# A 32 KB tile of normed activations moved from behind the weight buffers to the other end of SBUF

## The chip, the core and the metric

The kernel runs on one core of a Trainium2 chip, as one launch. The metric is the device time of that launch in microseconds. Three runs of the kernel before the change took 1527.56, 1529.47 and 1529.0 us; their median is 1529.0 us.

## What is computed

One decoder layer over 256 tokens of width 2048, in float32, cut to what matters here:

```
h    = RMSNorm(x)
proj = h @ w_in          # GDN q|k|v, beta, decay, out-gate z; attention q|k|v; gates A, B
y_a  = gated_deltanet(...) @ w_branch_a
y_b  = block attention(...) @ w_branch_b
x    = x + (sigmoid(gate_a) * y_a + sigmoid(gate_b) * y_b) @ w_out
h    = RMSNorm(x)
u    = causal_dwconv(h @ w_up)          # 2 x 5632 channels
x    = x + (silu(u_gate) * u_val) @ w_down
out  = RMSNorm(x)
```

Nearly all the arithmetic lies in the products with the weights: `w_in`, `w_branch_a`, `w_branch_b`, `w_out`, `w_up`, `w_down`.

## The kernel before

Activations stand transposed: channels on the 128 partitions, the 256 tokens along the free axis. Every float32 operand is split into a high and a low part in the type fp32r, and a product is the sum of high x high, high x low and low x high.

Weights come in blocks of 128 x 2048 numbers (1 MB). `fetch` (L120) lets SP issue the DMA into one of four `wraw` buffers; `load_w` (L125) lets ACT write the high part into one of two `wh` buffers (`split`, L118) and DVE the low part into one of two `wl` buffers (L115). These eight buffers of 8 KB in each partition are the pool `wpool`.

`block` (L168) multiplies a block of weights with an activation tile of the form [128, 16, 2, 256] (k-step, high or low, token). All its matmuls are issued at L108, in two forms:

- **Wide** (the gates from the fifth chunk on, the branches, the output projection, the up projection): for each k-step one matmul with `wh` as the stationary operand and the 512 columns high|low of the activations as the moving one, then one with `wl` and the 256 high columns. These two are called a pair below.
- **Narrow** (GDN, z, the attention's q and k, the first four gate chunks): three matmuls of 256 columns for each k-step.

Two products go the other way round, with the weights as the moving operand, 512 columns a time: the attention's v (`ps_v`, stationary `hc`) and the down projection (`pd`, L96, stationary `ah` and `al`, 128 columns a time).

The stages follow each other in this order: GDN, z and attention products with the delta rule and the attention running between them (`tick`, L103); gates (`ps_gate`); branches (`ps_br`, moving operands `yca` and `ycb`); output projection (`ps_wo`, moving operand `mc`); up projection (`ps_up`, moving operand `h2`); down projection (`pd`). The instructions are put in order by a scheduler when the program is built.

The tile in question is `hc` of the pool `hp` (L219, L220): 16 k-steps x 2 x 256 numbers, 32,768 bytes in each partition. It holds the normed input from the start until the gates are done. Under the same tag, and so at the same address, it is then `h2`, the normed input of the up projection, and at the very end `tail`, which holds the last two weight blocks of the down projection. The trace calls it `hc`, `h` and `tail`.

Pools stand as two stacks in SBUF. Without an argument a pool is put on the left stack, which grows upwards from low addresses: `keep`, `wpool`, `hp`, then `fk`, `m`, later `mp` (which holds `mc`), `b`, `b2` (which holds `ah`, `al` and the small tiles of the up projection). With `side="right"` it is put on the right stack, which grows downwards from the top: `n1`, `g`, `gp`, `yp` (`yca`, `ycb`), `bkeep`, `ak`.

## Time and profile before

| what | value |
|---|---|
| median of three runs | 1529.0 us (1527.56 to 1529.47) |
| span of the profiled execution | 1528.1 us |
| TensorE matmul (PE) busy | 1504.4 us, 98% |
| VectorE (DVE), ScalarE (ACT), GpSimd (POOL) busy | 67%, 49%, 12% |
| mean granted TensorE clock over the span | 0.997 |
| chain that ended last | PE 93%, of it `ps_up` 33%, `pd` 16%, `ps_gate` 11% |

The profile gives one execution, by its span from the first to the last instruction; that span is 0.9 us under the median of the three runs. Ends of matmuls are modelled in it and overlap the next one, so how fast matmuls follow each other is read from their starts, or from a long stretch and the number of matmuls in it. "PEld" is the load of a stationary operand.

### The profile page before, as it was taken

The numbers are of one execution on the slowest core, as the hardware profiler recorded it, in microseconds if no ns is written. First come the engines' busy times: TensorE is split into PE (matmuls) and PEld (weight loads), VectorE is DVE, ScalarE is ACT, GpSimd is POOL, SyncE is SP. The second block draws the span as 40 slices with busy tenths as digits, with TensorE's granted clock in tenths as the row PEclk, the third lists the DMA queues.
The fourth block names the chain that finished last, engine by engine and source line by source line (L and its number), as shares of the span: only waits on it lengthen the run. The fifth ranks groups of instructions, "written<-read, shape, count | busy, mean of one in ns | idle before, by whom it ended". The sixth has DMA issues, their size and how long they took to land.

```text
span 1528.1 us, 22511 instructions
## 1 busy us (share of the span) xinstructions
PE 1504.4 (98%) x9179; PEld 1343.1 (88%) x9179; DVE 1028.1 (67%) x1453; ACT 754.5 (49%) x1026; POOL 184.3 (12%) x137
## 2 busy tenths in 40 slices
PE   7999999999999999999999999999999999999997
PEld 6999999998998888888888888888888888888886
DVE  7887786886765555777766666766666676555554
ACT  5565463434474444445455545555455455444444
POOL 3001111041121000110101111111111111000000
PEclk9999999999999999999999999999999999999999
DMA  8454444444336553568545555555455554555552
GB/s 306 151 185 164 174 146 148 173 146 166 139 112 217 179 183 124 177 217 308 193 168 191 193 183 183 185 193 189 173 189 193 187 182 175 193 196 194 194 194 84
DMA packets 45639, 276.94 MB, mean 181 GB/s; under 512 B 5504, under 2 KB 6992, under 8 KB 15456
## 3 DMA queue, kind: packets, MB, share of 16 engines
q1 hardware_dynamic: 43712, 270.98, 49.8%
q0 software_dynamic: 960, 2.36, 0.6%
q10 hardware_dynamic: 864, 2.16, 0.4%
q8 instruction: 72, 1.18, 0.3%
q14 instruction: 31, 0.25, 0.0%
HBM read 271.68 MB, written 3.80 MB: 180 GB/s over the span
## 4 chain that ended last, share of the span: by engine, by line
PE 93%; DVE 4%; ACT 1%; issue 1%; DMA 0%; SPq 0%; DVEq 0%; ACTq 0%
PE ps_up L108 33%; PE pd L96 16%; PE ps_gate L108 11%; PE ps_gdn L108 9%; PE ps_wo L108 6%; PE ps_br L108 5%; PE ps_moba L108 4%; PE ps_z L108 3%; PE ps_v L108 3%; DVE wl L115 2%; ACT wh L118 1%; PE g L96 1%; PE py L545 1%; PE pu L551 1%; DVE tm L515 0%
## 5 line engine op out<-in xcount | busy, mean ns | idle before, releaser
L115 DVE TENSOR_TENSOR wl<-wraw,wh 128x1024 fp32r<-128x1024 f32 (+1 forms) x508 | 612.5, 1239 | 265.8 <-ACT wh L118 264.4
L118 ACT CAST wh<-wraw 128x1024 fp32r<-128x1024 f32 (+1 forms) x508 | 501.9, 1032 | 394.1 <-PE ps_up L108 126.8
L108 PE MATMUL ps_up<-h,wh 128*128 128x512 f32 x1408 | 497.9, 399 | 0.0
L108 PE MATMUL ps_up<-h,wl 128*128 128x256 f32 x1408 | 395.4, 281 | 0.0
L108 PEld LDWEIGHTS ps_up<-h,wh 128*128 128x128 f32 x1408 | 264.6, 188 | 66.1
L108 PEld LDWEIGHTS ps_up<-h,wl 128*128 128x128 f32 x1408 | 266.0, 189 | 0.1
L108 PE MATMUL ps_gate<-hc,wh 128*128 128x512 f32 (+1 forms) x640 | 183.1, 353 | 0.0
L108 PE MATMUL ps_gdn<-hc,wh 128*128 128x256 f32 x768 | 146.3, 291 | 7.5 <-ACT wh L118 5.8
L108 PE MATMUL ps_gate<-hc,wl 128*128 128x256 f32 x512 | 144.6, 282 | 0.6 <-DVE wl L115 0.6
L778 POOL TENSOR_TENSOR acts<-sg,cvf 128x256 f32<-128x256 f32 x44 | 80.8, 1837 | 432.6 <-ACT sg L777 432.6
L108 PEld LDWEIGHTS ps_gdn<-hc,wh 128*128 128x128 f32 x768 | 124.2, 198 | 8.5 <-ACT wh L118 5.8
L96 PE MATMUL pd<-wl,ah 128*128 128x512 f32 x336 | 130.8, 389 | 0.0
L96 PE MATMUL pd<-wh,al 128*128 128x512 f32 x336 | 130.8, 389 | 0.0
L108 PEld LDWEIGHTS ps_gate<-hc,wh 128*128 128x128 f32 x640 | 112.2, 189 | 18.0
L108 PE MATMUL ps_gdn<-hc,wl 128*128 128x256 f32 x384 | 111.7, 291 | 3.7 <-DVE wl L115 3.7
L772 ACT ACTIVATE cvf<-unf,ffv 128x256 f32<-128x256 f32 x88 | 48.2, 595 | 104.6 <-DVE unf L199 104.6
L774 DVE SCALAR_TENSOR_TENSOR cvf<-unf,ffv,cvf 128x254 f32<-128x254 f32 (+1 forms) x176 | 77.2, 480 | 32.2 <-ACT cvf L772 31.7
L108 PEld LDWEIGHTS ps_gate<-hc,wl 128*128 128x128 f32 x512 | 97.0, 189 | 0.8 <-DVE wl L115 0.8
L108 PE MATMUL ps_moba<-hc,wh 128*128 128x256 f32 x512 | 95.1, 285 | 0.0
L96 PE MATMUL pd<-wh,ah 128*128 128x512 f32 x336 | 92.8, 391 | 0.0
L108 PE MATMUL ps_wo<-mc,wh 128*128 128x512 f32 x256 | 88.8, 391 | 0.0
L108 PEld LDWEIGHTS ps_moba<-hc,wh 128*128 128x128 f32 x512 | 80.1, 191 | 0.2
(426 smaller groups left out, 2004.9 us busy)
## 6 DMA issues: line engine op xcount, KB each, us to landing
wraw<-in_w_up SPq DMA_DIRECT2D x88, 1024.0 KB, 4.8
wraw<-in_w_dn SPq DMA_DIRECT2D x44, 1024.0 KB, 4.8
wraw<-in_w_gate SPq DMA_DIRECT2D x32, 1024.0 KB, 4.8
wraw<-in_w_gdn SPq DMA_DIRECT2D x30, 1024.0 KB, 4.9
wraw<-in_w_moba SPq DMA_DIRECT2D x16, 1024.0 KB, 4.8
wraw<-in_w_o SPq DMA_DIRECT2D x16, 1024.0 KB, 4.8
wraw<-in_w_mv SPq DMA_DIRECT2D x8, 1024.0 KB, 4.8
wraw<-in_w_ba SPq DMA_DIRECT2D x16, 512.0 KB, 3.4
```

The costliest lines, as they stand in the source:

```text
L96: pe.matmul(ps, a, b, start=(start and i == 0), stop=(stop and i == n - 1), **kw)
L108: pe.matmul(ps, a, b, start=start, stop=stop, skip_group_check=True)
L115: (eng or dve).tensor_tensor(lo, src, hi.bitcast(F32), op=ALU.subtract)
L118: act.copy(hi, src)
L545: pe.matmul(py[:, p], ats[p], Tm[:, p], start=True, stop=True)
L551: pe.matmul(pu[:, p], Y[:, p, :], odd(U)[:, p], start=True, stop=True)
L772: act.activation(t[:, j, :], un[:, j, :], AF.Identity, scale=w[:, 2:3], bias=w[:, 3:4])
L774: dve.scalar_tensor_tensor(t[:, j, d:], un[:, j, :T - d], w[:, 2 - d:3 - d], t[:, j, d:], op0=ALU.mult, op1=ALU.add)
L778: pool.tensor_tensor(acts[:, c, :], sg, t[:, 1, :], op=ALU.mult)
```

## The change

The pool `hp` is put on the right stack, as the first pool there.

```diff
     hst = ExitStack()
-    hp = hst.enter_context(tc.tile_pool(name="hp", bufs=1))
+    hp = hst.enter_context(tc.tile_pool(name="hp", bufs=1, side="right"))
     hc = hp.tile([P, KD, 2, T], F32R, name="hc", tag="hc")
     hh, hl = hc[:, :, 0, :], hc[:, :, 1, :]
```

The other lines of the diff are comments that become empty lines; line numbers stay.

Both programs hold the same instructions in the same order on each engine, with the same waits. What differs are addresses. The pools that stood above `hp` on the left move down by its 32,768 bytes, and so do all pools of the right stack, which now begin below it. In bytes from the start of a partition:

| pool | tiles that matter here | before | after |
|---|---|---|---|
| `wpool` | `wraw` x4, `wh` x2, `wl` x2 | 18,624 to 84,160 | the same |
| `hp` | `hc`, `h2`, `tail` | 84,160 to 116,928 | 196,576 to 229,344 |
| `mp` | `mc` | 116,928 to 149,696 | 84,160 to 116,928 |
| `yp` | `yca`, `ycb` | 157,664 to 190,432 | 124,896 to 157,664 |
| `b2` | `ah`, `al` | 127,168 to 138,432 | 94,400 to 105,664 |
| `gp` | `gts` | 196,576 to 229,344 | 163,808 to 196,576 |

`wh` and `wl` lie at 51,392 to 84,160 in both programs. Every distance between two tiles stays what it was, except those to `hp` and, for tiles above it, those to `keep` and `wpool`.

## Rows read from the trace of the kernel before

**Rows 1.** Section 1 of the profile page: span, and busy time of each engine.

```profile
span 1528.1 us, 22511 instructions
PE 1504.4 (98%) x9179; PEld 1343.1 (88%) x9179; DVE 1028.1 (67%) x1453; ACT 754.5 (49%) x1026; POOL 184.3 (12%) x137
```

**Rows 2.** The chain of work that ended last, in order of time: start us, length us, engine, output tile, line, number of instructions.

```profile
347.73 10.00 PE ps_v L108 x44
...
455.13 141.46 PE ps_gate L108 x814
...
689.52 88.75 PE ps_wo L108 x512
779.14 4.86 PE ps_up L108 x28
784.86 492.54 PE ps_up L108 x2788
1285.77 234.67 PE pd L96 x1035
```

**Rows 3.** Busy time of each engine in 400 us of the up projection: stretch, its length, then PE, PEld, DVE, ACT and POOL, each with busy us and number of instructions, granted TensorE clock, DMA share, GB/s.

```profile
800.00:1200.00 400.00, 400.00 (x2266) 346.75 (x2265) 270.98 (x354) 205.64 (x286) 66.87 (x36) 1.00 0.52 187
```

**Rows 4.** The same view of 70 us of the output projection.

```profile
700.00:770.00 70.00, 70.00 (x405) 61.75 (x404) 49.89 (x54) 35.01 (x47) 7.47 (x5) 1.00 0.62 229
```

**Rows 5.** Groups of matmuls by shape: line, engine, output<-inputs, stationary, moving, count | busy us, mean ns of one (its end modelled) | idle us before them.

```profile
L108 PE MATMUL ps_up<-h,wh 128*128 128x512 f32 x1408 | 497.9, 399 | 0.0
...
L108 PE MATMUL ps_gate<-hc,wh 128*128 128x512 f32 x384 | 135.7, 399 | 0.0
...
L108 PE MATMUL ps_wo<-mc,wh 128*128 128x512 f32 x256 | 88.8, 391 | 0.0
...
L108 PE MATMUL ps_br<-yca,wh 128*128 128x512 f32 x128 | 44.7, 390 | 0.0
```

**Rows 6.** Timeline of PE in the up projection, the wide matmuls of four consecutive pairs and, three pairs on, one more: start us, modelled length us.

```profile
849.71 0.40 PE L108 MATMUL ps_up<-h,wh 128*128 128x512 f32 x1
...
850.05 0.40 PE L108 MATMUL ps_up<-h,wh 128*128 128x512 f32 x1
...
850.40 0.40 PE L108 MATMUL ps_up<-h,wh 128*128 128x512 f32 x1
...
850.77 0.40 PE L108 MATMUL ps_up<-h,wh 128*128 128x512 f32 x1
...
851.83 0.40 PE L108 MATMUL ps_up<-h,wh 128*128 128x512 f32 x1
```

**Rows 7.** The same for the output projection, four consecutive pairs.

```profile
739.63 0.39 PE L108 MATMUL ps_wo<-mc,wh 128*128 128x512 f32 x1
...
739.98 0.39 PE L108 MATMUL ps_wo<-mc,wh 128*128 128x512 f32 x1
...
740.33 0.39 PE L108 MATMUL ps_wo<-mc,wh 128*128 128x512 f32 x1
...
740.67 0.39 PE L108 MATMUL ps_wo<-mc,wh 128*128 128x512 f32 x1
```

**Rows 8.** Timeline of PE where the gates end and the branches begin.

```profile
595.02 0.40 PE L108 MATMUL ps_gate<-hc,wh 128*128 128x512 f32 x1
...
596.08 0.40 PE L108 MATMUL ps_gate<-hc,wh 128*128 128x512 f32 x1
...
596.43 0.40 PE L108 MATMUL ps_br<-yca,wh 128*128 128x512 f32 x1
...
596.78 0.39 PE L108 MATMUL ps_br<-yca,wh 128*128 128x512 f32 x1
...
597.82 0.39 PE L108 MATMUL ps_br<-yca,wh 128*128 128x512 f32 x1
```

**Rows 9.** Timeline of PE in a narrow stage, the attention's q and k: the last matmul of three consecutive k-steps (each has three matmuls of 256 columns).

```profile
260.12 0.28 PE L108 MATMUL ps_moba<-hc,wl 128*128 128x256 f32 x1
...
260.48 0.28 PE L108 MATMUL ps_moba<-hc,wl 128*128 128x256 f32 x1
...
260.84 0.28 PE L108 MATMUL ps_moba<-hc,wl 128*128 128x256 f32 x1
```

**Rows 10.** Timeline of PE in the product v where it is slowest: every third matmul.

```profile
278.24 0.39 PE L108 MATMUL ps_v<-wl,hc 128*128 128x512 f32 x1
...
278.94 0.39 PE L108 MATMUL ps_v<-wl,hc 128*128 128x512 f32 x1
...
279.63 0.39 PE L108 MATMUL ps_v<-wl,hc 128*128 128x512 f32 x1
...
280.32 0.39 PE L108 MATMUL ps_v<-wl,hc 128*128 128x512 f32 x1
```

**Rows 11.** One line of ACT, the copy of a 128x512 result out of PSUM into tiles of three pools: count, least/median/greatest ns, first and last start.

```profile
L196 ACT COPY unf<-ps_up x44: 571/577/580, 793.0 to 1279.2; 128x512 f32<-128x512 f32 x44
L196 ACT COPY bt<-ps_br x15: 573/580/582, 603.1 to 684.3; 128x512 f32<-128x512 f32 x15
L196 ACT COPY gts<-ps_gate x12: 573/579/581, 474.0 to 597.5; 128x512 f32<-128x512 f32 x12
```

## The prediction

> **What bounds the kernel now.** I read the busy times first: the matmul engine is busy 1504.4 of 1528.1 us, the next engine, DVE, 1028.1 [rows 1]. Then the chain that ended last: gates, output projection, up projection and down projection stand on it as long unbroken pieces of matmuls [rows 2]. [...] So the weights arrive in time there, and what counts is how fast one matmul follows the last. The change adds, removes and reorders no instruction; only if an address sets that pace can it move the time.

> So I compared the pace of stages that issue the same pair of matmuls, 512 columns with `wh`, then 256 columns with `wl`. From the chain [rows 2]: the up projection runs 2788 matmuls, 1394 pairs, in 492.54 us, **353.3 ns a pair**; the output projection 512 matmuls, 256 pairs, in 88.75 us, **346.7 ns a pair**. The groups by shape show the same seam: the 512-column matmul lasts 399 ns by the profile where the moving operand is `hc` or `h`, and 390 or 391 where it is `mc` or `yca` [rows 5]. The starts show how it comes about. In the up projection pairs follow each other after 0.34, 0.35 and 0.37 us, 1.06 us for three, and again 1.06 for the next three [rows 6]; in the output projection after 0.35, 0.35 and 0.34 us, 1.04 us for three [rows 7]. The seam lies at the tile, not at a pause: the last three gate pairs take 1.06 us (595.02 to 596.08), then the moving operand changes from `hc` to `yca` with PE running on, and three pairs from 596.78 to 597.82 take 1.04 us [rows 8].

> What is different between those stages? The weight buffers are the same, the shapes are the same, and the output projection has the other engines and the DMA about as busy (DVE 49.9 of 70 us, DMA share 0.62 against 0.52) [rows 3, 4]. What is left is the moving operand's place: `hc` and `h2` at 84,160, right behind `wpool`; `mc`, `yca` and `ycb` at 116,928 and above. The trace shows no cause beyond that, and one row speaks against it: the first 28 matmuls of the up projection, 14 pairs with `h2` at the same address, took 4.86 us, 347.1 ns a pair, up to 784.0 us, where a norm's matmuls step in and the slower pace begins [rows 2]. The place may only make the slow pace possible, and the way a stage is entered then decide.

> **The change part by part.** The profiled execution is the base: its span of 1528.1 us.

> *`hc` and `h2` at 196,576.* In the wide stages they are the moving operand of 1394 pairs of the up projection and of 384 pairs of the gates (x384 in [rows 5]). The least each can cost is the pace of `mc`, 346.7 ns; no row shows a faster pair, and the down projection's 512-column matmul (234.67 us for 1035, 226.7 ns [rows 2]) with the narrow stages' 256-column one (0.36 us for three, 120 ns [rows 9]) also add up to 346.7. The most is every pair as slow as the slowest of the three, 0.36 to 0.37 us by starts given to 0.01 us [rows 6]; at 0.36 that is 6.7 ns more than now, +11.9 us on 1778 pairs. I take the pace of `mc` and `yca`, because they are two tiles at two other places and both have it, and `ycb`, up to 190,432, is the nearest to the new place. That gives 1394 x 6.65 ns = 9.3 us and 384 x 6.65 ns = 2.5 us, together **-11.8 us**, all on the chain.

> *`mc` at 84,160, where `hc` was.* I charge it what `hc` pays there: 256 pairs x 6.65 ns = **+1.7 us**; ends 0 and, at 0.36 us a pair, +3.4.

> *`ah` and `al` at 94,400.* They are the stationary operand of the down projection's 1056 matmuls, with the weights moving, and now lie where `hc` lay. The nearest row is v, with `hc` stationary and the weights moving. At its slowest it took 2.08 us for nine matmuls, 231.1 ns [rows 10]; in a longer piece 10.00 us for 44, 227.3 ns [rows 2], which is the down projection's pace of today but for rounding. I take **0**; the bad end is 1056 x 4.4 ns = +4.7 us.

> *v and the narrow stages.* v has 192 matmuls with `hc`; between its two paces lie 192 x 4.4 ns = 0.8 us either way. The narrow stages already run at 120 ns, the floor worked out above, so I take **0** for them.

> *Everything else that moves.* ACT, DVE, POOL and DMA work with tiles 32,768 bytes lower. ACT's copy takes a median of 577, 580 and 579 ns into `unf` (left stack), `bt` and `gts` (right stack) [rows 11]: the place does not show. This work also lies beside PE. If PE gains 1.9% in the up projection, DVE's 271 us fall on 392 us instead of 400, and the output projection shows that weights can come faster (229 against 187 GB/s [rows 3, 4]), so the gain is not turned into a wait: **0**.

> Sum: -11.8 + 1.7 = -10.1 us, a span of 1518.0 us. The median of the runs is 0.9 us above the span of the profiled execution, so I predict **1519 us**. With the ends of `mc` and v in its favour it would be 1516.5; with the down projection's bad end 1523.7.

> [...]

> **The rivals.**

> *The place has no say.* The two paces would then be two ways in which the same stream of matmuls can run, chosen by how a stage begins. For it: the 347.1 ns at the start of the up projection, from the same address. Against it: the pace changes at `hc` to `yca` without a pause [rows 8], and the 1394 pairs after that start keep one pace for 492 us. Since the program's instructions and their order stay, each stage keeps its pace: 1529. [...]

> *The place allows it, the entry decides.* Then gates and up projection can part company at the new address. If only the up projection gets the fast pace, 1529 - 9.3 + 1.7 = 1521.4; if only the gates do, 1529 - 2.5 + 1.7 = 1528.2.

> *Slower: what moves in behind the weights pays, and `hc` is not relieved.* If the top of SBUF suits `hc` no better than its old place, nothing is gained, but `mc` pays 1.7 us and `ah` and `al` up to 4.7: 1529 + 6.4 = 1535.4. It decides once the down projection loses over 1.4 us (1.3 ns a matmul), since 1.7 + 1.4 is 0.2% of the time. Against it stand `yca` and `mc`, both fast at higher addresses, and v's return to 227 ns. If `hc` were to run worse there, up to 11.9 us would come on top.

> **How the numbers follow.** About 0.2%, 3 us, is what a measurement of this kernel can tell from no change. The forecast gets 0.58, the place without a say 0.24, the mixed case 0.08, half of it faster and half the same, the slower case 0.10. That makes faster 0.62, same 0.28, slower 0.10. The forecast's own range is 1516.5 to 1523.7. It holds too little alone; up to 1530, just above the slowest of the three runs, it takes in the cases of no change and the mixed ones, and leaves out the slower case: **1516.5 to 1530**.

> **What would show it.** Right: `ps_up` and `ps_gate` at 346.7 ns a pair, their 512-column matmul at 390 or 391 ns instead of 399, the piece of 2788 matmuls on the chain at about 483.3 us instead of 492.5; `ps_wo` up at 353 ns, 90.4 us for its 512; `pd` still at 226.7 ns. Wrong: `ps_up` still at 353.3 ns and 399 ns; or PE gaining there and idle before `ps_up` on `wl` by DVE, which would make DVE the bound I ruled out; or `pd` at 228 ns and more. Were `ps_up` relieved and `ps_wo` unchanged, the old place would not have been the cause, or not alone.

## The result: 1512 us, 1.1% faster than before

The changed kernel took 1512.2 us (median; 1511.06 to 1512.97), the kernel before 1529.1 us on the same chip; the ratio is 0.9894 (95% interval 0.9879 to 0.9908). The prediction was 1519 us with a range of 1516.5 to 1530: right in the sign and in the size of its largest term, but the gain that it gave is 7 us too small. Two executions in the whole record, 3829 us of the kernel before and 3008 us of e6_left128, were disturbed and stand in no ratio.

The profiled execution after the change has a span of 1510.8 us, 17.3 less than before. This is its page, as [rows 1]:

```profile
span 1510.8 us, 22511 instructions
PE 1487.7 (98%) x9179; PEld 1337.7 (89%) x9179; DVE 1027.2 (68%) x1453; ACT 754.6 (50%) x1026; POOL 184.9 (12%) x137
```

All of it is PE's: its busy time falls by 16.7 us, DVE's by 0.9. The chain after the change, beside [rows 2] (start us, length us, number of instructions):

```profile
105.33 11.20 PE ps_z L108 x96
...
342.42 10.25 PE ps_v L108 x44
...
449.36 138.81 PE ps_gate L108 x814
...
681.18 88.75 PE ps_wo L108 x512
770.80 4.86 PE ps_up L108 x28
776.52 483.26 PE ps_up L108 x2788
1268.14 235.03 PE pd L96 x1035
```

Read the starts against [rows 2]. The wide gates' piece starts 5.8 us earlier (455.13 to 449.36), the output projection 8.3 us earlier (689.52 to 681.18), the long piece of the up projection still 8.3 (784.86 to 776.52), the down projection 17.6 (1285.77 to 1268.14). So 5.8 us come from the stages before the wide gates, 2.6 from the wide gates and the branches, 0 from the output projection, 9.3 from the up projection, and the end gives 0.3 back. The 2788 matmuls of the up projection take 483.26 us, 346.7 ns a pair; the 96 of z take 11.20 us, 116.7 ns each. In the chain before, the same 96 took 120.0 ns each:

```profile
107.70 11.52 PE ps_z L108 x96
```

The groups by shape, as [rows 5], agree:

```profile
L108 PE MATMUL ps_up<-h,wh 128*128 128x512 f32 x1408 | 488.6, 390 | 0.0
...
L108 PE MATMUL ps_gate<-hc,wh 128*128 128x512 f32 x384 | 133.2, 390 | 0.0
```

And the narrow stage of [rows 9] on the timeline (start us, length us, engine, line), three k-steps of three matmuls each:

```profile
254.89 0.28 PE L108 MATMUL ps_moba<-hc,wl 128*128 128x256 f32 x1
...
255.24 0.28 PE L108 MATMUL ps_moba<-hc,wl 128*128 128x256 f32 x1
...
255.59 0.28 PE L108 MATMUL ps_moba<-hc,wl 128*128 128x256 f32 x1
...
255.94 0.27 PE L108 MATMUL ps_moba<-hc,wl 128*128 128x256 f32 x1
```

Here 0.35 us pass from k-step to k-step where 0.36 passed before.

### The profile page after: what moved, and what is told of

It is laid out like the page before. It is cut to its first block, busy times and chain, and to the rows that moved or that the text cites. A ratio compares the mean times of both kernels' runs of the same rounds, so it can differ in the third digit from the quotient of the medians.

```text
span 1510.8 us, 22511 instructions
## 1 busy us (share of the span) xinstructions
PE 1487.7 (98%) x9179; PEld 1337.7 (89%) x9179; DVE 1027.2 (68%) x1453; ACT 754.6 (50%) x1026; POOL 184.9 (12%) x137
## 4 chain that ended last, share of the span: by engine, by line
PE 93%; DVE 4%; ACT 1%; issue 1%; DMA 0%; POOL 0%; SPq 0%; DVEq 0%; ACTq 0%
PE ps_up L108 32%; PE pd L96 16%; PE ps_gate L108 11%; PE ps_gdn L108 9%; PE ps_wo L108 6%; PE ps_br L108 5%; PE ps_moba L108 4%; PE ps_z L108 3%; PE ps_v L108 3%; DVE wl L115 2%; ACT wh L118 1%; PE g L96 1%; PE py L545 1%; PE pu L551 1%; DMA wraw<-in_w_gdn 0%
## 5 line engine op out<-in xcount | busy, mean ns | idle before, releaser
L108 PE MATMUL ps_up<-h,wh 128*128 128x512 f32 x1408 | 488.6, 390 | 0.0
L108 PE MATMUL ps_gate<-hc,wh 128*128 128x512 f32 (+1 forms) x640 | 179.6, 347 | 0.0
L118 ACT CAST ah<-acts 128x256 fp32r<-128x256 f32 x44 | 17.9, 407 | 125.8 <-PE pd L96 116.1
```

The lines of the kernel that those rows point to most:

```text
L108: pe.matmul(ps, a, b, start=start, stop=stop, skip_group_check=True)
L118: act.copy(hi, src)
```

## The experiments

All kernels but one are the layer with unused bytes put ahead of or behind a tile; instructions and their order on each engine are the same in all of these. `pad(stack, name, bytes)` allocates a pool that nobody uses. The theory I held after seeing the result is A: not the place of `hc` counts but its start modulo a small number of bytes, relative to the weights. Before, `hc` and the weights start at the same value modulo 64 (and 256); after, `hc` starts 32 past them. P is the prediction's theory, that the place right behind the weights is to blame.

### e1_left32, hc stays behind the weights, 32 bytes on

```diff
-    hst = ExitStack()
-    hp = hst.enter_context(tc.tile_pool(name="hp", bufs=1))
+    hst = ExitStack(); pad(hst, "pa", 32)
+    hp = hst.enter_context(tc.tile_pool(name="hp", bufs=1)); pad(hst, "pb", 32)
```

> The kernel before, with 32 unused bytes ahead of hc and 32 behind it: hc stays on the left stack right behind the weight buffers, but starts at 84,192, which is 32 modulo 64, as the changed kernel's 196,576 is (before: 84,160, 0 modulo 64). All other tiles keep their start modulo 64; instructions and order stay. Theory A (the start modulo 64 decides): as the changed kernel, 1512 us, up projection 346.7 ns a pair, narrow matmuls 117 ns, v 233 ns. Theory P (the place behind the weights decides): as before, 1529 us, 353.3 ns, 120 ns, v 227 ns. Theory D (the distance from hc to the weight buffers, before a multiple of 8,192, decides): 1512 us as well, so e3 has to part it from A.

Measured: 1519.7 us, ratio 0.994 (0.9925 to 0.9955). Its chain (columns as above, and so in the chains below):

```profile
104.24 11.20 PE ps_z L108 x96
...
679.95 90.42 PE ps_wo L108 x512
...
776.96 483.25 PE ps_up L108 x2788
1268.61 241.38 PE pd L96 x1035
```

z and the up projection run as in the changed kernel, with `hc` still right behind the weights: P falls. But the time is not 1512 us, since two other stages lost: `ps_wo` 1.7 us, `pd` 6.3 (233.2 ns a matmul instead of 227.1). The two pads had moved `mc`, `ah` and `al` by 64 bytes, which I had taken for harmless. So 64 bytes count too, for other tiles as well.

### e2_right0, hc at the far end, 0 modulo 64

```diff
+    hst = ExitStack(); pad(hst, "pa", 32, side="right")
+    hp = hst.enter_context(tc.tile_pool(name="hp", bufs=1, side="right")); pad(hst, "pb", 32, side="right")
```

> The changed kernel, with 32 unused bytes ahead of hc and 32 behind it on the right stack: hc stays at the far end but starts at 196,544, 0 modulo 64. All other tiles keep their start modulo 64. Theory A: as the kernel before, 1529 us, 353.3 ns a pair in gates and up projection, narrow 120 ns, v 227 ns. Theory P: as the changed kernel, 1512 us. Theory D: 1512 us, since 196,544 is not a multiple of 8,192 away from the weights.

Measured: 1530.9 us, ratio 1.001 (0.9987 to 1.0033); three of its ten executions took 1521.4 to 1524.1 us, and the profile shows none of these. Its chain:

```profile
106.72 11.52 PE ps_z L108 x96
...
612.67 8.40 PE ps_br L108 x46
...
624.41 8.26 PE ps_br L108 x46
...
688.83 90.45 PE ps_wo L108 x512
780.14 4.86 PE ps_up L108 x28
785.87 492.54 PE ps_up L108 x2788
```

At the far end, but with the old start modulo 64, the old pace is back: 492.54 us, to the last digit that of [rows 2], and z at 120.0 ns. A holds, P is wrong on this side too. One row is new: `mc` lies at 84,160 here as it does in the changed kernel, with the same weights, and takes 90.45 us instead of 88.75. So the same two addresses give both paces.

### e3_left64, hc behind the weights, 64 bytes on

```diff
+    hst = ExitStack(); pad(hst, "pa", 64)
     hp = hst.enter_context(tc.tile_pool(name="hp", bufs=1))
```

> The kernel before, with 64 unused bytes ahead of hc: 84,224, still 0 modulo 64 and behind the weights, but no longer a multiple of 8,192 away from them. Theory A: 1529 us, 353.3 ns and 120 ns. Theory P: 1529 us. Theory D: 1512 us, 346.7 ns and 117 ns.

Measured: 1532.2 us, ratio 1.0032 (1.0017 to 1.0047). None of the three theories had it: z takes 11.31 us for 96 matmuls, 117.8 ns; the gates run at 348.9 ns a pair, the up projection at 353.3, and `pd`, whose `ah` and `al` moved by 64 as well, loses 6.3 us against the changed kernel. The chain:

```profile
105.96 11.31 PE ps_z L108 x96
...
451.14 139.66 PE ps_gate L108 x814
...
780.83 492.55 PE ps_up L108 x2788
1281.77 241.36 PE pd L96 x1035
```

Modulo 64 is therefore too short a rule; theory D (a multiple of 8,192) is out.

### e4_w32, the weights moved by 32 bytes

```diff
+    wst = ExitStack(); pad(wst, "pa", 32)
+    wpool = wst.enter_context(tc.tile_pool(name="wpool", bufs=2)); pad(wst, "pb", 32)
```

> The kernel before, with 32 unused bytes ahead of the weight buffers and 32 behind them: weights start at 32 modulo 64, hc at 84,224 (0 modulo 64). Theory A in its relative form (moving and stationary tile must start 32 apart modulo 64): gates and up projection 346.7 ns, narrow 117 ns, a gain of about 18 us there; the branches (yca and ycb at 32, as the weights now) may go from 346.7 to 353.3 ns, +1.7 us; v and the down projection, weights moving at 32 and stationary at 0, from 227 to 233 ns, +1.2 and +6.7 us; about 1520 us in all. Theory A in its absolute form (the moving tile's own start decides): hc as before, 353.3 and 120 ns; the weights as moving operand are now at 32, so v and the down projection may change in either direction; 1522 to 1536 us. Theories P and D: 1529 us and, by D, 1512 us.

Measured: 1519.3 us, ratio 0.9938 (0.9923 to 0.9953), as A's relative form had it. `hc`, at the same 84,224 as in e3_left64, is fast in the wide stages once the weights start 32 bytes before it modulo 256 (up projection 483.26 us against 492.55), so the distance between the two operands counts, not either start. `pd` loses 6.2 us (241.25 us). The narrow stages did not quite follow: these 96 matmuls of z take 11.31 us, 117.8 ns each, as in e3_left64, where 117 was expected.

```profile
104.93 11.31 PE ps_z L108 x96
```

The branches, whose operands are now 0 apart modulo 256, show in the chain how one distance had two paces:

```profile
587.64 13.77 PE ps_br L108 x79
604.80 8.40 PE ps_br L108 x46
616.54 8.41 PE ps_br L108 x46
628.34 8.27 PE ps_br L108 x46
640.07 8.27 PE ps_br L108 x46
```

Between these pieces PE waits a moment for `wl`, 0.29 us ahead of the one at 604.80. After one wait the same 46 matmuls take 8.40 us, after another 8.27, and no piece of 46 in this chain has a length between. The 0.13 us are 5.7 ns for each of the 23 pairs, most of the 6.6 between 353.3 and 346.7 ns. So my estimate, from these lengths, is that here the pace was chosen when the stream started again and kept nearly to the next stop. In [rows 8] it changes with the operands, 1.06 us for three pairs before and 1.04 after.

### b1_offsets, TensorE alone

```diff
+    rev(ws[0], 3)
+    for w in ws:
+        wide(w, 6)
+        narrow(w, 4)
+        rev(w, 6)
+    for w in ws:
+        narrow(w, 2)
+        wide(w, 6)
```

> Not the layer: TensorE alone, which runs the layer kernel's three kinds of product on 15 pairs of weight tiles that differ only in where they start, 0 to 224 bytes past a multiple of 256, while the activation tile stays at 128 past one. Output is a placeholder. For each pair: 48 wide pairs (512 and 256 columns, activations moving), 96 narrow matmuls (256 columns), 48 with the weights moving (512 columns); then in a second pass 48 narrow and 48 wide pairs again, so that wide is entered from another state. Theory A in its relative form (the distance from the stationary to the moving tile modulo 128 decides; runs of the layer so far: 0, 32 and 64): weights at 0 and at 128 give the same, wide 346.7 or 353.3 ns depending on how it is entered, narrow 120, weights moving 227; weights at 96 (activations 32 ahead) wide 346.7, narrow 117; weights at 64 wide 349 to 353, narrow 118, weights moving 233; distances under 32 bytes are open. If the distance modulo 256 counts, weights at 0 and 128 differ. Theory P (the place in SBUF decides): no pattern in the offset, a trend with the address, since the tiles lie one after the other from 49 KB to 180 KB.

Of the new kernel only the order of its products is shown. `ws` holds the 15 pairs of weight tiles; `wide`, `narrow` and `rev` issue the three forms, the last with the weights moving. The kernel leaves out all else of the layer, and its output means nothing. It ran once.

Worked out from the starts of the matmuls in the last two thirds of each group, to about 0.2 ns; d is the activations' start less the weights', modulo 256:

| d | wide pair, ns: pass 1, 2 | narrow, ns: pass 1, 2 | weights moving, ns |
|---|---|---|---|
| 0 | 353.6, 346.7 | 120.0, 120.0 | 226.7 |
| 16 | 346.7, 346.7 | 117.4, 119.9 | 236.8 |
| 32 | 346.7, 346.7 | 116.7, 116.7 | 233.3 |
| 48 | 350.0, 350.0 | 116.7, 116.7 | 230.0 |
| 64 | 353.4, 348.8 | 117.8, 117.8 | 233.4 |
| 80 | 349.2, 349.1 | 118.1, 118.1 | 231.2 |
| 96 | 350.0, 350.0 | 120.1, 119.9 | 234.3 |
| 104 | 350.1, 349.9 | 116.7, 117.9 | 233.4 |
| 112 | 349.2, 349.3 | 120.0, 120.0 | 233.3 |
| 120 | 348.9, 349.0 | 118.1, 118.0 | 233.3 |
| 124 | 353.4, 353.4 | 120.1, 118.7 | 236.0 |
| 128 | 351.2, 351.2 | 118.6, 119.9 | 232.2 |
| 160 | 346.6, 346.6 | 117.3, 118.7 | 233.3 |
| 192 | 353.4, 353.3 | 117.8, 113.4 | 233.4 |
| 224 | 353.6, 353.6 | 118.4, 118.4 | 233.3 |

The 5784 matmuls of the run stand on its chain as one unbroken piece of 935.33 us, and most paces of the layer are there at their distance: 0 (before), 32 (after), 64 (e3_left64, with both of its paces), 224 (the pieces of 8.40 us in the branches of e2_right0, whose pairs of 346 and 361 ns have a mean of 353). The table lacks the pieces of 8.26 us there, 346.7 ns a pair, and the 117.8 ns of e4_w32 at 32. d = 0 and d = 128 differ, so the distance counts modulo 256 and not 128. The tiles lie one after the other from 49 KB on, and no trend goes with that. At d = 0 the wide pairs took two paces in one execution, in pass 1 and then in pass 2 (the wide matmul of every third pair):

```profile
459.93 0.40 PE L41 MATMUL acc<-xb,wh_128b 128*128 128x512 f32 x1
...
460.99 0.40 PE L41 MATMUL acc<-xb,wh_128b 128*128 128x512 f32 x1
...
462.05 0.40 PE L41 MATMUL acc<-xb,wh_128b 128*128 128x512 f32 x1
```

```profile
869.77 0.39 PE L41 MATMUL acc<-xb,wh_128b 128*128 128x512 f32 x1
...
870.81 0.39 PE L41 MATMUL acc<-xb,wh_128b 128*128 128x512 f32 x1
...
871.85 0.39 PE L41 MATMUL acc<-xb,wh_128b 128*128 128x512 f32 x1
```

Three pairs take 1.06 us in the first, 1.04 in the second, as [rows 6] and [rows 7] do.

### e0_after and e7_left32c, the change against its offset alone

The next four kernels ran on one chip. The second of them leaves `hc` where it was but for 32 bytes, and keeps all other tiles at their old start modulo 256:

```diff
+    hst = ExitStack(); pad(hst, "pa", 32)
+    hp = hst.enter_context(tc.tile_pool(name="hp", bufs=1)); pad(hst, "pb", 224)
```

> The changed kernel itself, beside the next three on the same chip: 1512 us, up projection 346.7 ns a pair, narrow 117 ns, v 233 ns, down projection 227 ns.

> The kernel before, hc still on the left stack right behind the weight buffers, with 32 unused bytes ahead of it and 224 behind: hc starts 32 past the weights modulo 256, as in the changed kernel, and every other tile keeps its start modulo 256, which the kernel with 32 and 32 bytes did not. Theory A, now with 256 in place of 128 bytes: the changed kernel's time, 1512 us, with 346.7, 117, 233 and 227 ns in up projection, narrow stages, v and down projection, and the output projection at 346.7. Theory P (place): 1529 us.

Measured: the changed kernel 1511.8 us, ratio 0.9902 (0.987 to 0.9934); the kernel with 32 bytes of padding 1512.4 us, ratio 0.9906 (0.987 to 0.9942). The chain of the latter:

```profile
104.57 11.20 PE ps_z L108 x96
...
680.46 88.75 PE ps_wo L108 x512
770.07 4.86 PE ps_up L108 x28
775.79 483.26 PE ps_up L108 x2788
1267.42 235.03 PE pd L96 x1035
```

These are the lengths of the changed kernel, piece by piece. The whole gain is the 32 bytes; the move to the other end adds nothing that these runs can tell. From the first `wh` to `hc` it is 145,184 bytes in the changed kernel and 32,800 here: both are 32 modulo 256, but 288 and 32 modulo 512, so the period is not 512 either.

### e6_left128

The same edit with 128 and 128 bytes.

> The kernel before, with 128 unused bytes ahead of hc and 128 behind: hc starts 128 past the weights modulo 256, all other tiles as before. If the distance counts modulo 128, this is the kernel before: 1529 us, 353.3 ns a pair, narrow 120, v 227. If it counts modulo 256, this is the measurement of TensorE alone at 128: wide 351.2 ns, narrow 118.6 to 120, v 232; about 1527 us.

Measured: 1524.1 us, ratio 0.9975 (0.9959 to 0.9991), where about 1527 was expected. Its chain:

```profile
104.80 11.39 PE ps_z L108 x96
...
343.96 10.22 PE ps_v L108 x44
...
780.04 489.45 PE ps_up L108 x2788
```

489.45 us for 1394 pairs is 351.1 ns, z 118.6 ns, v slower than its 10.00 us of [rows 2]: the table's line 128, not line 0. The rule is modulo 256 in the layer too.

### e5_two, hc and h2 at two distances

```diff
-    hc = hp.tile([P, KD, 2, T], F32R, name="hc", tag="hc")
+    hpt = lambda n, o: hp.tile([P, 8256], F32R, name=n, tag="hc")[:, o:o + 8192]; hc = hpt("hc", 40).rearrange("p (k a t) -> p k a t", a=2, t=T)
...
-    h2 = hp.tile([P, KD, 2, T], F32R, name="h2", tag="hc")
+    h2 = hpt("h2", 0).rearrange("p (k a t) -> p k a t", a=2, t=T)
...
-    tail = hp.tile([P, 2, 2, 2048], F32R, name="tail", tag="hc")
+    tail = hpt("tail", 0).rearrange("p (a b n) -> p a b n", a=2, b=2)
```

> The changed kernel, with hc 192 past the weights modulo 256 in the narrow stages, v and the gates, while h2 and tail stay at 32. By TensorE alone, where narrow ran at 117.8 ns in the first pass and 113.4 in the second at this distance: narrow 113.4 ns, a gain of 2688 x 3.3 = 9 us, or 117.8, a loss of 3 us, by how the stage is entered; the wide gates 353.4 ns, a loss of 2.6 us; up projection 346.7 as in the changed kernel. 1506 to 1518 us. Theory P: 1512 us, the change moves tiles by 256 bytes alone.

Measured: 1510.3 us (1506.7 to 1511.5), ratio 0.9889 (0.9852 to 0.9927); its profiled execution spans 1504.6 us, that of e0_after 1509.2. Its chain:

```profile
101.66 10.88 PE ps_z L108 x96
...
335.06 10.07 PE ps_v L108 x44
...
440.75 141.17 PE ps_gate L108 x814
...
770.26 483.26 PE ps_up L108 x2788
```

z at 113.3 ns a matmul, the gates 2.4 us slower than in the changed kernel (138.81), as the table has it for d = 192; v, at 229 ns, fits it less well (233). It has the lowest median of all, by 1.5 us, but its interval overlaps that of e0_after, so a gain is not shown. Its runs spread over 5 us where those of e0_after spread over 2, as they would if the narrow pace of 113 or 118 ns were again chosen at the entry; the profile shows only one of them.

## Why the prediction was right where it was, and where it failed

*PE bounds, and an address sets its pace.* Right. PE is busy through the 400 us of [rows 3]. The seam of [rows 8] lies at the tile, and moving that tile moved the pace of the up projection and the gates: 9.3 and 2.6 us measured, 9.3 and 2.5 predicted, the long piece at 483.26 us for 483.3. That these two came out so close is luck. They were argued from the new place, and e2_right0, at the same end of SBUF, has none of this gain; the tile happened to come to lie 32 bytes past the weights modulo 256.

*The narrow stages are at a floor of 120 ns.* This is the step that failed, and it makes most of the error. The stages before the wide gates gained 5.8 us though v in them lost; most narrow matmuls went to 116.7 ns, some to 117.8. Worked out from the starts in both traces, from 30 us on, the 2458 narrow matmuls that follow another one directly take 294.3 us before and 287.3 after, 7.0 less; v takes back 1.0 of it, longer waits of PE another 1.0, and PE's other steps there gain 0.8. I had built the floor from sums: 346.7 less 226.7 gave 120 and fitted. But two paces at a distance of 0 do not bound a third one, and the trace before already spoke against the sum: in the pairs of its output projection the wide matmul takes 230.1 ns from its start to the next one, and the one of 256 columns 116.6 (means). b1_offsets has 113.4 ns for a narrow matmul.

*`mc` pays 1.7 us at `hc`'s old address.* Wrong in the changed kernel: 88.75 us, as before. It does pay in e2_right0 (90.45 us). At distance 0 both paces exist. What chooses is not settled; the branches ahead of `mc` lie at distance 32 in the changed kernel, where only the fast pace was seen (8.26 or 8.27 us for each piece of 46), and run mixed at distance 224 in e2_right0 (8.26 and 8.39 or 8.40 us), so the entry may differ by them; but the last 31 matmuls ahead of `mc` took 5.59 us in both, the fast pace. The 14 fast pairs at the start of the up projection, which I gave as evidence against the place, fit the same two paces.

*v within 0.8 us.* It lost about 1 us (its two paces of [rows 2] and [rows 10], 227.3 and 231.1 ns, are 3.8 ns apart, not the 4.4 of the sum, and the new pace, 233 ns, lies outside them): 10.25 instead of 10.00 us for 44, and 0.2 us in the piece of 40. Its operands were at distance 0, the best in b1_offsets for the form with the weights moving (226.7 ns), and left it for 32 (233.3 ns). *The down projection: 0.* Right (235.03 and 234.67 us); its operands kept their distance.

*The cause.* The prediction blamed the place right behind the weights. e1_left32, e2_right0 and e7_left32c show that the place has no say, at both ends of SBUF: what counts is the distance between moving and stationary operand modulo 256 bytes (up projection: 353.3 ns a pair at 0, 346.7 at 32, 351.1 at 128), and at some distances how the stream is entered (output projection at 0: 88.75 or 90.45 us). TensorE alone, in b1_offsets, runs the same pair in 346.6 to 353.6 ns by the distance of its own two operands. The rival that the place has no say was right in that and wrong in its 1529 us, since the move changed the distance. The rival of the mixed case was half right, for `mc` and for distance 0.

*What stays open.* What it is in the chip that has a period of 256 bytes. Whether the moving operand's distance to the weights of its own matmul counts, or to those of the next one: `wh` and `wl` always lay at the same distance. And why the kernel before took 1519.3 to 1521.5 us in 6 of its 32 executions beside the experiments with the layer, as e2_right0 did in 3 of 10 (to 1524.1): an up projection that entered at the fast pace would save 9.3 us, which fits, but no profile caught one. In both kernels `h2` lies at distance 0. In 21 executions of the five runs with `hc` and `h2` at distance 32 (the changed kernel twice, e1_left32, e4_w32, e7_left32c) there was no such jump; none of the five spreads over more than 3.3 us. Those 6 executions of the kernel before widen the intervals of the experiments' ratios.

## What to carry to other kernels

Where TensorE is busy all the time, compare the start-to-start pace of stages that issue the same matmuls; a difference that follows a tile and no engine (here 353.3 against 346.7 ns a pair, 2%) pointed to the addresses of its two operands. Then try 32 bytes of padding before moving anything (in e7_left32c they were the whole gain), and keep every other pair of operands at its distance modulo 256, or one stage pays for another, as the down projection did with 6.3 us in e1_left32. A pace that one stage shows is not a floor until it has been seen to hold at other distances: 120.0 ns for narrow matmuls at distance 0 was 116.7 at 32.
